# A two-layer encoder on one core: bias diagonals laid out during the value chunks, value loads and the last head's mixing placed differently

## The chip, the core and the metric

The kernel runs on one core of a Trainium2 chip. The metric is the device time of one execution in microseconds (us). The engines are PE (matrix multiplications and transposes into PSUM banks), DVE and POOL (elementwise work), ACT (activations, copies; it also issues DMAs from its own queue) and SP (issues DMAs only). Each engine executes its instructions in the order in which the program hands them over.

## What is computed

S = D = 1024, one batch, fp32. Each layer is `x <- x + RMSNorm_post(mixer(RMSNorm_pre(x)))`. Layer A is the part that the change touches, with 16 heads of width 128 and chunks of 128 positions:

```
z = h @ w_in                        # (1024, 3*2048)
u, v, g = split(z, 3)
u = gelu(u)
v = layer_norm(gelu(v), vn_g, vn_b)
vc = v.reshape(chunks, 128, 16, 128)
sg = einsum('hpq,cqhd->cphd', w_s, vc) + b_s    # mixing of positions
y = u * sg * silu(g)
return y @ w_out
```

Layer B is dilated window attention with a relative-position bias. The bias of a (query, key) pair depends on their distance alone, so the kernel makes one vector `vec` per head and lays it out 128 times in DRAM tensors `toep0`, `toep1`, `toep2`, from which layer B later reads diagonals.

## The kernel before

Products of fp32 values are made of three matmuls on high and low parts ("hi", "lo"). Weights come through `Pieces`: SP loads a 128 x 512 piece into `raw` (L160), ACT copies the hi part into one of 8 buffers `wt` (L176), and DVE or POOL subtracts for the lo part (L178). Nearly every matmul has the line L270, activations have L285, two-operand DVE and POOL work L288, fused DVE work L291.

The order of all work is written out by hand. `Plan` is a heap of steps with due times; its clock `plan.now` advances with each matmul by a modelled duration, and after each matmul of `dmm` all steps that are due are emitted, on whichever engine they belong to. `plan.after(dt, f)` places a step `dt` modelled microseconds ahead.

The stages, in real time of the profiled execution:

- 0 to 64: normalisation, and chunk 0 of the values (columns 0 to 511 of v). 64 to 202: value chunks 1 to 3, 8 pieces of weights each; their ends lie near 118, 163 and 203. At a chunk's end ACT evacuates eight PSUM banks into `vst` tiles (5 buffers) and SP stores each to `va` in DRAM (`va<-vst`, L107, 256 KB each).
- Into the chunks and the heads after them go 12 fills (`toep_fill`, L511): ACT issues one DMA, DRAM to DRAM, for four heads of one `toep` tensor: 768 KB (toep0), 1536 KB (toep1) or 512 KB (toep2).
- 202 to 555: 16 heads. Each head multiplies seven forms (a11, a12, s2, s1, s3, a22, s4) in that order; the weights of head h+1 are loaded in head h by `w_load` (L572): four SP loads `wb<-in_a_w_in` (b11, b21, b12, b22), then `w_sum` on POOL (t1 = b12 - b11, and three more), then hi and lo parts as pieces. Results are copied from PSUM by ACT (tiles `p`, `u`).
- Beside the multiplications of head h+1 runs the spatial part of head h: SP loads its values, 512 KB (`vr<-va`, L690), and the position weights come on ACT's queue (`wsr` L667, `bsr` L669); ACT normalises the values (L285, `vr`), ACT and DVE split them (`vs`), PE mixes in four steps (`mix`, `psS<-wst,vs`), DVE forms `sg` and `ya` (L291, L288), and SP stores `ya<-ya` (L725).
- From 555: the first output projection, whose pieces alternate between `ya` and `w_out`; the mixing of the last head lies in it. Then layer B, from 755 to the end.

Every SP or ACT transfer is assigned one of eight completion counters, in turn over both queues (`DMAHW0` to `DMAHW7` in the rows of the instruction order). An issue waits until the transfer that had its counter last has landed.

The steps that the change touches, with the lines of before:

```
plan.after(20.0 + 30.0 * (g + 3 * (h // 4)), toep_fill, g, h)   # the 12 fills
if pc.split < 32 + 7 * h:                                       # w_load
plan.at(t0, v_load)                                             # spatial
plan.at(t0 + 3.5 + 0.35 * i, v_norm, i)
plan.after(14.0, lambda: [f() for f in mixes])                  # last head
```

Of the kernel before, what the change touches and what calls it, by code (L numbers as in the profile page):

```python
# [12 lines left out]
F32 = mybir.dt.float32  # L13
# [8 lines left out]
P = 128  # L22
# [196 lines left out]
def encoder_block(ctx: ExitStack, tc: tile.TileContext, x, norm_pre, norm_post, a_w_in, a_w_s,  # L219
                  a_b_s, a_vnorm_g, a_vnorm_b, a_w_out, b_w_in, b_w_out, rel_bias, sel, out):  # L220
    nc = tc.nc
# [6 lines left out]
    plan = Plan()  # L228
# [12 lines left out]
    pc = Pieces(nc, plan, lambda: wpool.tile([P, 2, 512], F32R, name="wt"), 8)  # L241
# [136 lines left out]
    va = dram.tile([NH, P, 8, P], F32, name="va")  # L378
# [96 lines left out]
    for i in range(8):  # L475
        b = bank("D")
        for k in range(8):
# [5 lines left out]
            while n > 0 and norms:  # L483
                weight, f = norms.pop(0)
# [29 lines left out]

    for g in range(3):
        for h in range(0, NH, 4):
            plan.after(20.0 + 30.0 * (g + 3 * (h // 4)), toep_fill, g, h)

# [40 lines left out]

    def w_load(h):

        if pc.split < 32 + 7 * h:
            plan.after(0.5, w_load, h)
            return
        cols = a_w_in.shape[-1]
        B = {}
        for f, j, c0 in (("b11", 0, 128 * h), ("b21", 1, 128 * h), ("b12", 0, 2 * W2 + 128 * h),
                         ("b22", 1, 2 * W2 + 128 * h)):  # L570
            B[f] = fm.tile([P, 512], F32, name="wb", bufs=6)
            nc.sync.dma_start(B[f].rearrange("p (k n) -> p k n", k=4),  # L572
                              bass.AP(tensor=a_w_in.tensor, offset=a_w_in.offset + j * 512 * cols + c0,
                                      ap=[[cols, P], [128 * cols, 4], [1, 128]]))
        plan.after(3.0, lambda: w_sum(h, B, 0))
# [14 lines left out]
    for k in range(4):  # L590
        T = {}
# [32 lines left out]
    sp = sps.enter_context(tc.tile_pool(name="sp", bufs=2, side="right", reuse_waits="tile"))  # L624
# [35 lines left out]
    ws = {}  # L660

    def ws_load(h):

        if h < NH:
# [3 lines left out]
            T["b"] = sp.tile([P, P], F32, name="bsr")  # L668
            nc.scalar.dma_start(T["b"], bcast_row(a_b_s, h * P, P))  # L669

    def spatial(h, ug, t0):
        vs, T = {}, ws.pop(h)

        def ws_tr():
            b = bank("T")
            tr(b[:, :128], T["w"])
            T["wt"] = sp.tile([P, 2, P], F32R, name="wst")
            act(T["wt"][:, 0], b[:, :128])
            tt(T["wt"][:, 1], b[:, :128], T["wt"][:, 0].bitcast(F32), OP.subtract)

        def ws_sum():
            b = bank("T")
            bmm(b[:, :256], ones, T["wt"].rearrange("p a q -> p (a q)"), True, True)
            T["t2"] = sp.tile([P, P], F32, name="t2")
            stt(T["t2"], b[:, :128], vgb[:, 1, h:h + 1], T["b"], OP.mult, OP.add)
            stt(T["t2"], b[:, 128:256], vgb[:, 1, h:h + 1], T["t2"], OP.mult, OP.add)

        def v_load():
            vs["r"] = sp.tile([P, 8, P], F32, name="vr", bufs=1)
            nc.sync.dma_start(vs["r"], va[h])  # L690

        def v_norm(i):
            act(vs["r"][:, i], vs["r"][:, i], AF.Identity, scale=lnr[:, i:i + 1], bias=lnb[:, i:i + 1])

        def v_split(e):
            if e == 0:
                vs["v"] = sp.tile([P, 2, 8, P], F32R, name="vs", bufs=1)
                act(vs["v"][:, 0], vs["r"])
            else:
                tt(vs["v"][:, 1], vs["r"], vs["v"][:, 0].bitcast(F32), OP.subtract)  # L700

        def mix(cc):
            b = bank("S")
            for k in range(2):
                c = 2 * cc + k
                bmm(b[:, 256 * k:256 * k + 256], vs["v"][:, 0, c], T["wt"].rearrange("p a q -> p (a q)"),
                    True, False)
                bmm(b[:, 256 * k:256 * k + 256], vs["v"][:, 1, c], T["wt"].rearrange("p a q -> p (a q)"),
                    False, True)
            g = sp.tile([P, 2, P], F32, name="sg")  # L710
            b4 = b.rearrange("p (c a q) -> p c a q", c=2, a=2)
            t2 = T["t2"][:, None, :].to_broadcast([P, 2, P])
            stt(g, b4[:, :, 0], vgb[:, 0, h:h + 1], t2, OP.mult, OP.add)
            stt(g, b4[:, :, 1], vgb[:, 0, h:h + 1], g, OP.mult, OP.add)

            if cc == 0:
                vs["y"] = sp.tile([P, S], F32, name="ya", bufs=1)
            y = vs["y"].rearrange("p (t c b) -> p c t b", t=8, c=8)[:, 2 * cc:2 * cc + 2]
            tt(y, g.rearrange("p c (b t) -> p c t b", t=8),
               ug[:, 256 * cc:256 * cc + 256].rearrange("p (c b t) -> p c t b", c=2, t=8), OP.mult)  # L720
            if cc == 3:
                plan.after(2.0, y_out)

        def y_out():
            nc.sync.dma_start(ya[h], vs["y"])  # L725
            done_a.add(h)
            pc.pump()

        plan.at(t0, v_load)
        plan.at(t0 + 0.2, ws_tr)  # L730
        for i in range(8):
            plan.at(t0 + 3.5 + 0.35 * i, v_norm, i)
        plan.at(t0 + 6.5, v_split, 0)
        plan.at(t0 + 7.6, v_split, 1)
        plan.at(t0 + 6.2, ws_sum)
        plan.at(t0 + 7.6, ws_load, h + 2)
        return mix
# [68 lines left out]
    def head(h, mixes):  # L806
        if h + 1 < NH:
            plan.after(0.8, w_load, h + 1)
        u = sp.tile([P, S], F32, name="us")
        c0, c1 = slice(0, 512), slice(512, 1024)  # L810
        x, z, y = bank("D"), bank("O"), None
        g = {}

        def snap(nm):
            g[nm] = sp.tile([P, 512], F32, name=nm, bufs=1)
            act(g[nm], x)

        def gate(c, o, nm):

            g[c] = g[nm]  # L820
            tt(g[c], o, g[nm], OP.add)

        def gated(c, i):
            tt(u[:, c], u[:, c], g[i], OP.mult)

        form_mm(x, "a11", True)
        snap("p1")
        form_mm(z, "a12", True)
        tt(u[:, c0], z, g["p1"], OP.add)
        form_mm(x, "s2")  # L830
        snap("u2")
        y = bank("O")
        form_mm(y, "s1", True)
        form_mm(x, "s3")
        snap("u3")
        gate(1, y, "u3")
        for f in mixes[:2]:
            f()
        form_mm(x, "a22")
        act(u[:, c1], x, AF.Gelu_apprx_tanh)  # L840
        act(u[:, c0], u[:, c0], AF.Gelu_apprx_tanh)
        for f in mixes[2:3]:
            f()
        form_mm(y, "s4")
        gate(0, y, "u2")
        for f in mixes[3:]:
            f()
        for dt, c in ((0.0, 1), (0.9, 0)):
            plan.after(dt, act, g[c], g[c], AF.Silu)
        plan.after(1.4, gated, c1, 1)  # L850
        plan.after(2.4, gated, c0, 0)
        mix = spatial(h, u, plan.now + 0.5)
        return [lambda cc=cc: mix(cc) for cc in range(4)]

    mixes = []
    for h in range(NH):
        mixes = head(h, mixes)
    plan.after(14.0, lambda: [f() for f in mixes])
    fms.close()
    rps = ExitStack()  # L860
    rp = rps.enter_context(tc.tile_pool(name="rp", bufs=6, reuse_waits="tile"))
# [769 lines left out]
```

## Time and profile before

| what | value |
| --- | --- |
| median of three runs | 1989.4 us (1987.28 to 1990.86) |
| profiled execution | 1986.57 us |
| its span | 1984.8 us |
| PE busy | 1942.6 us, 98% |
| DVE, ACT, POOL busy | 67%, 55%, 17% |
| chain that ended last | PE 85%, DVE 6%, DMA 3%, ACT 3% |
| mean granted TensorE clock | 0.994 |

The views used are: the waits (which line of an engine stood idle for what, in total, how many times and the longest), the timeline of one engine in a window (start, duration, operation and, in brackets, the idle time ahead with what ended it), the chain of work that ended last, followed back from the end, a table by stretch of time (busy time of each engine, granted clock, DMA share and rate), and the DMA rate in slices of a window.

### The profile page before, as it was taken

Reading aid. Unit: us, or ns where it says so; the run is one execution under the profiler, and the core shown is the slowest. Engines: PE = TensorE matmul, PEld = TensorE weight load, DVE = VectorE, ACT = ScalarE, POOL = GpSimd, SP = SyncE. Lnnn points to the kernel's source line nnn. Section 1 sums busy time; section 2 is a strip of 40 time slices with the busy share of each in tenths; the row PEclk is TensorE's granted clock in tenths of the full one; section 3 lists DMA queues with packets and bytes.
Section 4 is the critical chain, followed back from the end, with each engine's and each line's share of the span. In section 5 each row is a group of like instructions: output and inputs, shape, how many; then the busy total and the mean of one; then the engine's idle time right before and its main releaser. Section 6 shows DMA issues by size and latency. Waiting matters only on the chain.

```text
span 1984.8 us, 30678 instructions
## 1 busy us (share of the span) xinstructions
PE 1942.6 (98%) x10617; PEld 1660.8 (84%) x10617; DVE 1326.7 (67%) x3051; ACT 1101.0 (55%) x2455; POOL 337.3 (17%) x394
## 2 busy tenths in 40 slices
PE   8999999999999999999999999999999999999998
PEld 5888787888778889988888888888888988787876
DVE  6455787888764777146576675676775756868647
ACT  5322566666645564246655656556556565675722
POOL 0001332232100000001131031120211300324032
PEclk9999999999999999999999999999999999999999
DMA  5342543443256775222232241322322322313277
GB/s 179 103 123 90 168 143 123 140 133 112 85 189 204 231 220 181 80 62 75 67 98 76 77 121 54 95 84 75 107 76 72 110 71 79 99 56 100 91 231 268
DMA packets 246024, 235.57 MB, mean 119 GB/s; under 512 B 18843, under 2 KB 203835, under 8 KB 245868
## 3 DMA queue, kind: packets, MB, share of 16 engines
q1 hardware_dynamic: 235068, 219.97, 36.2%
q10 hardware_dynamic: 10800, 13.63, 2.0%
q8 instruction: 84, 1.38, 0.3%
q14 instruction: 72, 0.59, 0.1%
HBM read 188.03 MB, written 57.04 MB: 123 GB/s over the span
## 4 chain that ended last, share of the span: by engine, by line
PE 85%; DVE 6%; DMA 3%; ACT 3%; issue 1%; POOL 1%; SPq 0%; ACTq 0%; DVEq 0%; POOLq 0%
PE psD L270 57%; PE psO L270 13%; PE psS L270 8%; PE psT L281 4%; PE psT L270 3%; DVE wt L178 1%; DVE o L288 1%; DMA vr<-va 1%; DMA va<-vst 0%; ACT wt L176 0%; DVE sg L291 0%; DMA raw<-in_b_w_in_dram 0%; DMA ya<-ya 0%; DVE xs L1157 0%; POOL o L288 0%
## 5 line engine op out<-in xcount | busy, mean ns | idle before, releaser
L270 PE MATMUL psD<-hTh,wt 128*128 128x512 f32 x2176 | 722.4, 396 | 5.7 <-ACT u L285 5.5
L270 PEld LDWEIGHTS psD<-hTh,wt 128*128 128x128 f32 x2176 | 401.1, 189 | 73.9 <-ACT u L285 6.6
L270 PE MATMUL psD<-hTl,wt 128*128 128x512 f32 x1088 | 433.1, 398 | 0.0
L270 PE MATMUL psD<-wt,hTh 128*128 128x256 f32 (+1 forms) x1760 | 357.1, 299 | 3.2 <-DVE wt L178 2.4
L178 DVE TENSOR_TENSOR wt<-raw,wt 128x512 fp32r<-128x512 f32 x316 | 210.1, 699 | 155.7 <-ACT wt L176 154.4
L270 PEld LDWEIGHTS psD<-wt,hTh 128*128 128x128 f32 x1760 | 281.9, 191 | 15.5 <-DVE wt L178 3.6
L285 ACT ACTIVATE xs<-xs,st 128x256 f32<-128x256 f32 (+2 forms) x384 | 176.7, 461 | 174.2 <-DVE st L1157 173.2
L176 ACT ACTIVATE wt<-raw 128x512 fp32r<-128x512 f32 x328 | 191.3, 624 | 144.3 <-PE psD L270 50.0
L270 PE MATMUL psD<-wt,hTl 128*128 128x256 f32 (+1 forms) x880 | 263.9, 300 | 0.8 <-DVE hTl L288 0.8
L270 PEld LDWEIGHTS psD<-hTl,wt 128*128 128x128 f32 x1088 | 205.3, 189 | 33.5
L270 PEld LDWEIGHTS psD<-wt,hTl 128*128 128x128 f32 x880 | 167.5, 190 | 6.3 <-DVE hTl L288 1.9
L288 DVE TENSOR_TENSOR pt<-psT,pt 128x512 fp32r<-128x512 f32 (+1 forms) x192 | 115.1, 600 | 85.5 <-ACT pt L285 82.8
L1157 DVE CUSTOM_DVE_ANT_0 xs<-psS,bias 128x256 f32<-128x256 f32 (+1 forms) x256 | 95.9, 412 | 61.6 <-PE psS L270 59.5
L1083 POOL TENSOR_SCALAR ks<-ks 64x512 fp32r<-64x512 f32 x96 | 59.6, 620 | 427.4 <-ACT ks L285 423.6
L288 DVE TENSOR_TENSOR ks<-psD,ks 64x512 fp32r<-64x512 f32 x96 | 66.1, 689 | 79.3 <-ACT ks L285 77.7
L270 PEld LDWEIGHTS psO<-pt,vs 128*128 128x128 f32 (+1 forms) x640 | 99.2, 177 | 23.5 <-DVE pt L288 7.2
L270 PE MATMUL psO<-pt,vs 128*128 128x256 f32 (+1 forms) x640 | 107.9, 282 | 4.6 <-DVE pt L288 3.5
L270 PE MATMUL psS<-ks,qs 128*128 128x256 f32 x640 | 109.8, 286 | 0.0
L285 ACT ACTIVATE pt<-psT 128x512 fp32r<-128x512 f32 (+1 forms) x192 | 99.9, 520 | 14.5 <-PE psT L281 11.6
L281 PE MATMUL psT<-ident,xs 128*128 128x128 f32 x640 | 103.6, 274 | 3.4 <-ACT xs L285 2.5
L270 PEld LDWEIGHTS psS<-ks,qs 128*128 128x128 f32 x640 | 97.9, 189 | 10.2 <-DVE ks L288 0.2
L285 ACT ACTIVATE ks<-psD 64x512 fp32r<-64x512 f32 x96 | 57.0, 593 | 80.7 <-PE psD L270 79.1
(218 smaller groups left out, 3191.3 us busy)
## 6 DMA issues: line engine op xcount, KB each, us to landing
raw<-in_b_w_in_dram SPq DMA_DIRECT2D x160, 256.0 KB, 3.0
wb<-in_a_w_in_dram SPq DMA_DIRECT2D x64, 256.0 KB, 6.4
raw<-ya SPq DMA_DIRECT2D x64, 256.0 KB, 3.0
raw<-in_a_w_out_dram SPq DMA_DIRECT2D x64, 256.0 KB, 4.0
y<-yd SPq DMA_DIRECT2D x56, 256.0 KB, 5.6
cb<-sc SPq DMA_DIRECT2D x64, 192.0 KB, 4.9
raw<-in_a_w_in_dram SPq DMA_DIRECT2D x32, 256.0 KB, 3.5
va<-vst SPq DMA_DIRECT2D x32, 256.0 KB, 3.9
```

Source lines behind the costliest of these rows:

```text
L176: self.nc.scalar.activation(hi, src, AF.Copy)
L178: e.tensor_tensor(lo, src, hi.bitcast(F32), op=OP.subtract)
L270: nc.tensor.matmul(o, l, r, start=start, stop=stop, skip_group_check=more)
L281: nc.tensor.transpose(o, i, ident)
L285: nc.scalar.activation(o, i, f, **k)
L288: (e or nc.vector).tensor_tensor(o, a, b, op=op)
L1083: nc.gpsimd.tensor_scalar(place(u, u.k[a][:, 0], o, o + 64, hh), hi.bitcast(F32), 1.0, 0.0, op0=OP.mult, op1=OP.add)
L1157: nc.vector.tensor_tensor_reduce(out=o, in0=s_, in1=bi, op0=OP.add, op1=OP.min, scale=1.0, scalar=3.0e38, accum_out=col(0, t))
```

## The change

Four edits. The 12 fills get due times 10 + 11.5 n after the start of chunk 1 in place of 20 + 30 n, so all of them are due within 136.5 modelled microseconds. `w_load` no longer waits for the pieces ahead of it where h is 0. The load of a head's values moves out of `spatial` into `head`, due 12 modelled microseconds after the head's start, and the normalisation and splitting of the values come 1.3 sooner. The last head's mixing is due 19 in place of 14 after the head's end.

```diff
-            plan.after(20.0 + 30.0 * (g + 3 * (h // 4)), toep_fill, g, h)
+            plan.after(10.0 + 11.5 * (g + 3 * (h // 4)), toep_fill, g, h)
...
-        if pc.split < 32 + 7 * h:
+        if h and pc.split < 32 + 7 * h:
...
+    vr = {}
+
+    def v_load(h):
+        vr[h] = sp.tile([P, 8, P], F32, name="vr", bufs=1)
+        nc.sync.dma_start(vr[h], va[h])
+
     def spatial(h, ug, t0):
-        vs, T = {}, ws.pop(h)
+        vs, T = {"r": vr.pop(h)}, ws.pop(h)
...
-        def v_load():
-            vs["r"] = sp.tile([P, 8, P], F32, name="vr", bufs=1)
-            nc.sync.dma_start(vs["r"], va[h])
...
-        plan.at(t0, v_load)
         plan.at(t0 + 0.2, ws_tr)
         for i in range(8):
-            plan.at(t0 + 3.5 + 0.35 * i, v_norm, i)
-        plan.at(t0 + 6.5, v_split, 0)
-        plan.at(t0 + 7.6, v_split, 1)
+            plan.at(t0 + 2.2 + 0.35 * i, v_norm, i)
+        plan.at(t0 + 5.2, v_split, 0)
+        plan.at(t0 + 6.3, v_split, 1)
...
     def head(h, mixes):
         if h + 1 < NH:
             plan.after(0.8, w_load, h + 1)
+        plan.after(12.0, v_load, h)
...
-    plan.after(14.0, lambda: [f() for f in mixes])
+    plan.after(19.0, lambda: [f() for f in mixes])
```

What the edits do to the order of instructions on each engine:

On ACT, at the end of value chunk 3 and the start of head 0, there stood before (the evacuations of the last two banks, the first form's copies, the position weights' loads, the copies of head 0):

```order
L285 ACTIVATE vst<-psD 128x512 [waits DMAHW5_49,DVE_49,PE_49]
L285 ACTIVATE vst<-psD 128x512 [waits DMAHW6_49,DVE_49,PE_49]
L285 ACTIVATE hTh<-s_699 128x512 x4
L667 DMA wsr<-in_a_w_s_dram 128x128
L669 DMA bsr<-in_a_b_s_dram 128x128
L667 DMA wsr<-in_a_w_s_dram 128x128 [waits DMAHW0_49]
L669 DMA bsr<-in_a_b_s_dram 128x128 [waits DMAHW2_49]
L285 ACTIVATE p_1656<-psD 128x512 [waits PE_49]
```

and now there stands, with the eleventh of the twelve fills, a toep1 of 1536 KB, in it:

```order
L285 ACTIVATE vst<-psD 128x512 [waits DMAHW3_49,DVE_49,PE_49]
L285 ACTIVATE vst<-psD 128x512 [waits DMAHW4_49,DVE_49,PE_49]
L511 DMA toep_99<-vec 512x1x768 [waits DMAHW0_49]
L285 ACTIVATE hTh<-s_699 128x512 x4
L667 DMA wsr<-in_a_w_s_dram 128x128
L669 DMA bsr<-in_a_b_s_dram 128x128 [waits DMAHW5_49]
L667 DMA wsr<-in_a_w_s_dram 128x128 [waits DMAHW7_49]
L669 DMA bsr<-in_a_b_s_dram 128x128 [waits DMAHW1_49]
L285 ACTIVATE p_1663<-psD 128x512 [waits PE_49]
```

Behind it only one more fill is left (toep2, in head 0); before, eight fills lay at or behind this place, in the heads.

On SP, from the last store of chunk 3 to the first value load, there stood before (`wb` are the four loads of head 1's weights):

```order
L107 DMA va<-vst 128x4x128 [waits DMAHW3_49,Activation_49]
L628 DMA vrow<-in_a_vnorm_g_dram 16x128 [waits DMAHW5_49]
L629 DMA vrow<-in_a_vnorm_b_dram 16x128 [waits DMAHW7_49]
L572 DMA wb<-in_a_w_in_dram 128x4x128 [waits DMAHW1_49]
L572 DMA wb<-in_a_w_in_dram 128x4x128 [waits DMAHW3_49]
L572 DMA wb<-in_a_w_in_dram 128x4x128 [waits DMAHW4_49,DVE_49,Pool_49]
L572 DMA wb<-in_a_w_in_dram 128x4x128 [waits DMAHW5_49,DVE_49,Pool_49]
L690 DMA vr<-va 128x1024 [waits DMAHW2_49,DMAHW6_49,DMAHW0_49,DVE_49]
```

and now:

```order
L107 DMA va<-vst 128x4x128 [waits DMAHW2_49,Activation_49]
L628 DMA vrow<-in_a_vnorm_g_dram 16x128 [waits DMAHW4_49]
L629 DMA vrow<-in_a_vnorm_b_dram 16x128 [waits DMAHW6_49]
L572 DMA wb<-in_a_w_in_dram 128x4x128 [waits DMAHW0_49]
L572 DMA wb<-in_a_w_in_dram 128x4x128 [waits DMAHW2_49]
L572 DMA wb<-in_a_w_in_dram 128x4x128 [waits DMAHW3_49,DVE_49,Pool_49]
L572 DMA wb<-in_a_w_in_dram 128x4x128 [waits DMAHW4_49,DVE_49,Pool_49]
L675 DMA vr<-va 128x1024 [waits DMAHW5_49,DMAHW1_49,DVE_49]
```

The transfers are the same and in the same order; the counters have shifted. The first load of head 1's weights now waits on counter 0, which the fill of ACT's row above was the last to be given; before it waited on counter 1, which a store of chunk 3 had last. The value loads of heads 0 to 13 and the loads of head 0's weights stand at the same places as before; the value load of head 14 stands one transfer sooner, that of head 15 six `raw` loads sooner.

On PE, in the first output projection, the last head's mixing (`psS<-wst,vs`) moves behind 24 more matmuls of the projection:

```order
+L270 MATMUL psD<-wt 128x512 x6
+L270 MATMUL psO<-wt 128x512 x6
+L270 MATMUL psD<-wt 128x512 x6
+L270 MATMUL psO<-wt 128x512 x6
L270 MATMUL psD<-wt 128x512 x4
L270 MATMUL psS<-wst,vs 128x256 x16
L270 MATMUL psD<-wt 128x512 x2
-L270 MATMUL psO<-wt 128x512 x6
-L270 MATMUL psD<-wt 128x512 x6
-L270 MATMUL psO<-wt 128x512 x6
-L270 MATMUL psD<-wt 128x512 x6
```

No other matmul changes its place. POOL's order is unchanged; on DVE four `wt` subtractions of the projection now stand ahead of the last head's `sg` steps.

## Rows read from the trace of the kernel before

**Rows 1.** The page: busy time of the engines.

```profile
PE 1942.6 (98%) x10617; PEld 1660.8 (84%) x10617; DVE 1326.7 (67%) x3051; ACT 1101.0 (55%) x2455; POOL 337.3 (17%) x394
```

**Rows 2.** PE's waits: total us, times, longest us.

```profile
PE psD L270 <- ACT u L285: 5.5, 3, 2.6
...
PE psD L270 <- ACT vst L285: 0.7, 2, 0.5
```

**Rows 3.** PE's timeline at the three waits for `u`: start, us, operation [idle before].

```profile
219.15 0.50 PE L270 MATMUL psD<-hTh,wt 128*128 128x512 f32 x1 [1.29 <-ACT u L285]
...
329.28 0.50 PE L270 MATMUL psD<-hTh,wt 128*128 128x512 f32 x1 [2.56 <-ACT u L285]
...
544.42 0.50 PE L270 MATMUL psD<-hTh,wt 128*128 128x512 f32 x1 [1.69 <-ACT u L285]
```

**Rows 4.** ACT's timeline in head 5, around a fill.

```profile
314.81 0.61 ACTq L511 DMA_DIRECT2D toep<-vec  x1
...
320.23 4.67 ACTq L667 DMA_DIRECT2D wsr<-in_a_w_s_dram  x1
```

**Rows 5.** The chain, 300 to 352: start, us, what.

```profile
329.28 4.38 PE psD L270 x12
...
348.93 2.77 PE psD L270 x12
```

**Rows 6.** By stretch: PE, PEld, DVE, ACT, POOL busy; clock, DMA share, GB/s.

```profile
330.00:335.00 5.00, 5.00 (x18) 4.05 (x18) 4.60 (x10) 2.35 (x4) 0.00 (x0) 0.66 0.40 139
575.00:580.00 5.00, 4.47 (x14) 3.79 (x15) 4.76 (x10) 0.00 (x0) 0.00 (x0) 0.52 0.55 174
```

**Rows 7.** The chain in head 14: the value load, and PE's piece after the third wait.

```profile
534.67 4.39 DMA vr<-va
...
544.42 3.04 PE psD L270 x12
```

**Rows 8.** SP's waits, whole span: what the `raw` load ahead of it waited for.

```profile
SPq L160 <- DVE wst L288: 20.3, 1, 20.3
```

**Rows 9.** PE's timeline around the last head's mixing.

```profile
569.58 0.28 PE L270 MATMUL psS<-wst,vs 128*128 128x256 f32 x1
570.52 1.09 PE L270 MATMUL psS<-wst,vs 128*128 128x256 f32 x7 [0.67 <-DVE vs L288]
575.14 1.19 PE L270 MATMUL psS<-wst,vs 128*128 128x256 f32 x4 [3.53 <-DVE sg L291]
...
580.51 1.54 PE L270 MATMUL psD<-wt 128*128 128x512 f32 x6
```

**Rows 10.** DVE's timeline in the same stretch.

```profile
570.39 3.69 DVE L178 TENSOR_TENSOR wt<-raw,wt 128x512 fp32r<-128x512 f32 x6
574.00 0.48 DVE L291 SCALAR_TENSOR_TENSOR sg<-psS,vgb,t 128x256 f32<-128x256 f32 x1
...
575.03 0.63 DVE L288 TENSOR_TENSOR ya<-sg,us 128x256 f32<-128x256 f32 x1
```

**Rows 11.** The chain at the ends of chunks 2 and 3: the stores.

```profile
155.11 6.89 DMA va<-vst
...
199.12 2.84 DMA va<-vst
...
202.07 0.60 ACT vst L285
```

**Rows 12.** The chain in head 0, from head 1's third weight load on.

```profile
209.51 3.40 DMA wb<-in_a_w_in_dram
```

**Rows 13.** DMA rate, 219 to 243, 0.6 us a slice, behind a fill issued at 219.57.

```profile
GB/s 0 0 51 271 155 103 77 97 87 102 108 108 108 102 102 102 108 102 102 102 108 108 108 102 102 102 119 182 128 135 93 187 260 373 341 334 351 300 212 160
```

**Rows 14.** SP's waits, 330 to 350, and its store of `ya` there.

```profile
SPq L725 <- DMA toep<-vec: 8.6, 1, 8.6
SPq L725 <- DVE wst L288: 3.2, 1, 3.2
...
340.53 0.34 SPq L725 DMA_DIRECT2D ya<-ya  x1
```

## The prediction

> **What bounds the kernel now.** The page first: PE is busy for 98% of the span [rows 1], so a change that removes no matmul can gain no more than PE's idle and slow-clocked pieces. Next the view of PE's waits, for what is idle in layer A: 5.5 us in three waits for ACT's copies `u`, and 0.7 us for `vst` at the ends of the value chunks [rows 2]. PE's timeline puts the three at 219.15 (1.29 us, head 0), 329.28 (2.56 us, head 5) and 544.42 (1.69 us, head 14) [rows 3]. The last head's mixing, at 570 to 580, is the fourth place, with waits of 0.67 and 3.53 us [rows 9]. Then the chain at each place, for what released it, and the table by stretch for the clock: behind two of these places it was granted at 0.66 and 0.52 on the mean of 5 us, a mixture of its two levels of 1.2 and 2.4 GHz, after stretches in which PE had stood idle [rows 6]. In the heads PE otherwise runs at 1.00 without gaps; the weights, values and position weights arrive behind it.
>
> **Part 1, fills out of the heads: the gain.** In head 5 ACT issued a fill at 314.81, and its next DMA issue, `wsr` at 320.23, then held ACT's queue for 4.67 us [rows 4]. Behind it stood the copies of weights and then `u`, for which PE waited 2.56 us [rows 3]. The 12 matmuls after that took 4.38 us, and the same 12 one head later 2.77 [rows 5]; the 1.61 between is the clock at 0.66. With no fill in head 5 both go: 2.56 + 1.61 = 4.2 us. Nothing is late next there, since the other heads without a fill at that place show no such wait in [rows 2].
>
> **Part 2, value loads.** The order of SP's transfers is unchanged through head 13, so "values sooner" and "first weights sooner" cost and gain nothing there. In head 14 the value load, 4.39 us long [rows 7], stood behind a `raw` load that waited 20.3 us [rows 8]; ACT's normalisation came late from it and `u` behind that, 1.69 us of PE [rows 3]. It now stands ahead of that load: 1.69 gone, and the 12 matmuls lose 3.04 - 2.77 = 0.27 us less (the piece at 544.42 [rows 7] against its usual length [rows 5]): 2.0 us. Normalising 1.3 sooner moves ACT work among ACT work with the same length: nothing.
>
> **Part 3, the last mixing.** From 569.58 to 580.51, 10.93 us, PE did 16 mixing matmuls and 8 of the projection [rows 9]. At full clock these take 16 x 0.12 + 8 x 0.2275 = 3.74 us (0.12 and 0.2275: 12 projection matmuls take some 2.75 us [rows 5], and mixing matmuls have half their columns). So 7.2 us are lost, idle and clock together. The 3.53 us are six `wt` subtractions of 3.69 us that DVE did ahead of the first `sg` [rows 10]. Moved 24 matmuls (5.5 us) later, the values are split well before the mixing and PE has no 0.67 us wait. What stays: PE can be two steps ahead of DVE (two banks psS), and one step is 0.48 + 0.48 + 0.63 us on DVE [rows 10] against 0.48 us on PE, so the third step waits for an `sg` pair (about 0.5 after PE's own second step), the fourth a further 1.1, and one or two subtractions may still be queued ahead (up to 1.0). That is 2.6 us left, 4.6 gained; between 1.5 (five subtractions ahead again) and 7.
>
> Gains together: 4.2 + 2.0 + 4.6 = **10.8 us**, 7.7 to 13.
>
> **Part 4, the ends of chunks 1 and 2: a cost.** Twelve fills now run nearly back to back from chunk 1 to head 0, since one alone moves at 102 to 108 GB/s [rows 13]. Beside a fill the store that frees the `vst` buffer took 6.89 us at the end of chunk 2, without one 2.84 us at the end of chunk 3 [rows 11]. The four microseconds showed as 0.7 us on PE in two waits [rows 2], since PE works on banks that are free. By the new order single stores of chunk 1 and of chunk 2 also wait for a fill's landing by its counter, which no row of before shows at this place. From below it costs nothing, if the fills have landed by then; from above a few us at each end, 5 together, as `SPq L725` once waited 8.6 us for a fill [rows 14]. I take the middle, **2.5 us**. The Trainium skill, "DMA: Bandwidth & Descriptors", section "Issuing engines are not separate DMA queues", says that transfers started by different engines run on the same 16 DMA engines and interleave; it speaks against moving fills beside stores, and were it not so this term would be nothing and the sum 2.5 us smaller. The two store durations side with it.
>
> **Part 5, head 0: the main cost.** The eleventh fill, 1536 KB, now stands on ACT's queue right behind the last `vst`, which in before ended at 202.07 + 0.60 [rows 11]; with the 2.5 us of part 4 and some queueing it is issued at about 206 (203 to 207). On SP the first load of head 1's weights is given the counter that this fill had last, and so waits until it has landed. Such a wait is real: in head 5's end the store `ya<-ya`, which neither reads nor writes `toep`, waited 8.6 us for a fill, and 3.2 us more for `wst`, before it was issued at 340.53; so the fill issued at 314.81 landed at 337.3, after 22.5 us [rows 4, 14]. From below: 1.573 MB at 105 GB/s is 15.0 us, and some 1.5 us pass before the rate rises [rows 13], so 16.5. The new place lies between: little else runs beside it while SP waits, but the last stores do. I take 19, landing at 225 (219.5 to 229.5).
>
> Behind the waiting load on SP stand the other three weight loads and head 0's values. POOL needs the third (b12); it is issued about 1.0 us after the first, lands after 3.4 us [rows 12], and from that landing, 209.51 + 3.40 = 212.91, to PE's a22 matmul at 219.15 [rows 3] there were 6.24 us of POOL differences, ACT copies and `u`. PE's order is fixed, so a22 of head 0 starts at 225 + 1.0 + 3.4 + 6.2 = 235.6 in place of 219.15: 16.4 later, of which 2.5 are part 4's. **+14 us** (11.5 to 17.5, by the fill's two lengths). Position weights that queue on ACT behind the fill, up to 4.67 us each [rows 4], lie inside this wait.
>
> The clock falls after so long a wait. What followed the 2.56 us wait cost 1.6 us (part 1); 5 us at 0.52, as behind the mixing [rows 6], would be 5 x 0.48 = 2.4. **+2.0 us**.
>
> Costs together 18.5 us, 13 to 25. The sum: -10.8 + 18.5 = **+7.7 us**, on the profiled execution 1986.6 + 7.7 = 1994.3. The profiled execution lies 2.8 us under the median, so the median would be 1989.4 + 7.7 = **1997.1 us**.
>
> **The rivals.**
>
> *Faster: the fill has landed when SP comes to the load.* Mechanism: counter 0 is free before head 1's weights are due. In before, SP came to its first weight load by about 207, and a delay of the third is covered only as far as POOL's wait allows; the 1.29 us wait at 219.15 [rows 3] says that there is no slack. So it decides at a landing by about 208 to 209; each later microsecond is one of PE. Then costs are part 4 and perhaps 1 us: -10.8 + 2.5 + 1 = -7.3, **1982 us** (1978 to 1985). For it: ACT could reach the fill sooner, and its rate could be higher when no head runs. Against it: every slice of a fill alone shows 102 to 108 GB/s [rows 13]; a landing at 208 from 203 needs three times that. 0.12. The Trainium skill gives this result by a formula ("DMA: Bandwidth & Descriptors", section "Anatomy of one DMA — SWDGE (gpsimd) path"): a DMA takes 2.0 us plus its bytes by 436e3 per us, an estimate of 5.6 us for this fill. The trace has three to four times as much.
>
> *No change: the gain and the stall cancel.* A fill of 16.5 us issued at 203, and no cost at the chunk ends: landing 219.5, PE at 230.1, +11 us, with 1.6 for the clock 12.6, less 10.8 to 13: **1990 us** (1986 to 1993). It needs all bounds on one side. 0.18.
>
> *It doesn't do what it says.* "Weights and values sooner" is empty in the order through head 13; that is in the sum already. The fills and the mixing do move.
>
> **How the numbers follow.** A difference under 0.2% (4 us) is about what a measurement of this kernel can't tell from none: faster is below 1985.4, slower above 1993.4. Forecast (slower) 0.70, its own range 1992 to 2006: gains from -12 to -8, costs 15 to 25. The other two 0.18 and 0.12. The range of 8 in 10, 1988 to 2006, leaves out the faster rival and the far end of the stall.
>
> **What the profile after would show.** Part 5 right: PE's waits have `psD <- ACT u` with a longest wait of 11 to 17 us in head 0, SP's waits have `L572 <- DMA toep<-vec`, and a slow clock stands behind it; POOL's first difference of head 1 starts at about 229. Wrong: that wait is near 1 us. Parts 1 and 2: no wait for `u` in heads 5 and 14. Part 3: the `sg` waits under 3 us and the clock near 1 behind the mixing. Part 4: `vst` waits of 1 to 5 us in all. The prediction is wrong above all if the weight load of head 1 isn't held, or if the fills delay each other so that the eleventh lands after 230.

## The result, and the profile after

The changed kernel takes 2001.08 us (median of 4 runs, 2000.61 to 2002.7), the kernel before 1988.39 us in the same series (4 runs, 1987.28 to 1990.86). The ratio is 1.006 with a 95% interval of 1.0048 to 1.0072: slower by 12.7 us. The forecast was 1997.1 us, 1988 to 2006, slower.

To see where the time went, the same PE instruction is looked up in both traces, stage by stage. The difference of its two start times is what the changed kernel has lost up to there.

| PE instruction | before | after | lost so far | in this stage |
| --- | --- | --- | --- | --- |
| first matmul of chunk 1 | 70.59 | 69.93 | -0.7 | |
| second piece of chunk 2 | 119.55 | 121.79 | +2.2 | +2.9 (end of chunk 1) |
| first matmul of head 0 | 201.82 | 207.92 | +6.1 | +3.9 (end of chunk 2) |
| transpose of head 0's position weights | 226.27 | 249.09 | +22.8 | +16.7 (head 0) |
| the same of head 5 | 338.38 | 356.95 | +18.6 | -4.2 (heads 1 to 5) |
| the same of head 15 | 555.67 | 572.62 | +17.0 | -1.6 (heads 6 to 15) |
| second part of the first projection | 607.73 | 619.99 | +12.3 | -4.7 (last mixing) |
| layer B, first group | 910.25 | 922.33 | +12.1 | -0.2 |
| end of the span | 1984.8 | 1999.4 | +14.6 | +2.6 |

Of the gain in heads 1 to 5, -4.4 us lie in head 5, and of that in heads 6 to 15, -1.9 lie in head 14; each of the other heads takes 0.03 us longer than before. ("Head 14" is, as in the prediction, the stretch around 544 in which the values of head 14 are worked on; PE is at the forms of the last head there.) Up to layer B this adds to 12.7 us from the start of chunk 1. That is the difference of the medians; the last 2.6 us of the profiled executions come almost wholly in the last 75 us and are taken up at the end.

The view of PE's waits after the change (what waited, for what: us in all, times, longest) answers to [rows 2]:

```profile
PE psD L270 <- ACT p L285: 7.9, 1, 7.9
PE psD L270 <- ACT u L285: 7.4, 1, 7.4
...
PE psD L270 <- ACT vst L285: 3.6, 4, 1.8
...
PE psS L270 <- DVE sg L291: 2.1, 2, 1.2
```

The waits for `u` in heads 5 and 14 are gone, `sg` lost nearly half. In their place stand 15.3 us in head 0, in two waits, and 3.6 us for `vst` (and 0.6 more in front of bank psO) where there were 0.7. SP's waits name what it waited for at the weight loads of heads 0 and 1:

```profile
SPq L572 <- DMA toep<-vec: 19.1, 2, 17.2
```

The chain of work through head 0 (start, us, what):

```profile
208.18 20.89 DMA toep<-vec
...
229.51 3.40 DMA wb<-in_a_w_in_dram
...
234.38 1.09 POOL tw L288
...
239.02 0.60 ACT u L285
...
239.67 5.49 PE psD L270 x12
```

It reads as part 5 put it: the fill is issued at 208.18 and lands at 229.07, then the weight loads go out, 3.40 us for the third of them, POOL's differences, the copies, `u`, and PE's a22 at 239.67. The forecast had 206, 225 and 235.6. ACT's timeline shows the first of PE's two waits:

```profile
208.18 0.60 ACTq L511 DMA_DIRECT2D toep<-vec  x1
...
209.23 8.28 ACTq L667 DMA_DIRECT2D wsr<-in_a_w_s_dram  x1
...
220.92 0.60 ACT L285 ACTIVATE p<-psD 128x512 f32<-128x512 f32 x1 [9.89 <-DMA bsr<-in_a_b_s_dram]
```

The load of `wsr` behind the fill held ACT's queue for 8.28 us (4.67 in [rows 4]), so `p` came late and PE stood; the work it did between that wait and the next shortened the second wait. By stretch (the number after POOL's is the clock), both waits are followed by matmuls at about the lower level of the clock, 1.2 GHz:

```profile
221.00:226.00 5.00, 4.43 (x12) 3.53 (x13) 0.69 (x1) 0.52 (x1) 0.00 (x0) 0.56 0.31 115
226.00:231.00 5.00, 5.00 (x23) 3.77 (x21) 0.00 (x0) 0.60 (x1) 0.00 (x0) 1.00 0.27 87
...
240.00:245.00 5.00, 5.00 (x13) 3.84 (x13) 3.32 (x4) 0.55 (x1) 1.39 (x1) 0.50 0.39 127
```

At the ends of chunks 1 and 2 the chain goes through a store that took 8.29 and 9.09 us, where [rows 11] had 6.89 and, without a fill beside it, 2.84:

```profile
111.95 8.29 DMA va<-vst
```

```profile
157.42 9.09 DMA va<-vst
```

Behind the second of them the clock was low for some 3 us (by stretch):

```profile
167.00:170.00 3.00, 2.74 (x7) 2.16 (x8) 2.58 (x4) 0.84 (x3) 0.00 (x0) 0.56 0.51 159
```

### The profile page after: what moved, and what is told of

Read it like the earlier page. It is cut to its first block, busy times and chain, and to the rows that moved or that the text cites. A ratio compares the mean times of both kernels' runs of the same rounds, so it can differ in the third digit from the quotient of the medians.

```text
span 1999.4 us, 30674 instructions
## 1 busy us (share of the span) xinstructions
PE 1944.7 (97%) x10617; PEld 1660.7 (83%) x10617; DVE 1320.9 (66%) x3051; ACT 1103.2 (55%) x2455; POOL 338.4 (17%) x394
## 4 chain that ended last, share of the span: by engine, by line
PE 86%; DVE 5%; DMA 5%; ACT 2%; issue 1%; POOL 1%; SPq 0%; DVEq 0%; ACTq 0%; POOLq 0%
PE psD L270 57%; PE psO L270 13%; PE psS L270 8%; PE psT L281 4%; PE psT L270 3%; DMA toep<-vec 1%; DMA va<-vst 1%; DMA y<-yd 1%; DVE wt L178 1%; DVE o L288 1%; DMA raw<-in_b_w_in_dram 1%; DMA raw<-in_a_w_in_dram 0%; DVE xs L1159 0%; DMA cb<-sc 0%; DVE qs L291 0%
## 5 line engine op out<-in xcount | busy, mean ns | idle before, releaser
L270 PEld LDWEIGHTS psD<-wt,hTh 128*128 128x128 f32 x1760 | 282.3, 191 | 18.4 <-ACT vst L285 6.0
```

Of the source, the lines that this page charges most:

```text
L270: nc.tensor.matmul(o, l, r, start=start, stop=stop, skip_group_check=more)
```

## The experiments

All twelve kernels are compared with the kernel before in series of their own, in which its median was 1986.8 to 1987.2 us. The table gives, by stage and against the trace of before, what each lost or gained, and the difference of the medians. "Chunk ends" is all that lies between the first matmul of chunk 1 and that of head 0; the columns of head 5 and head 14 hold that one head alone. A stage in which the clock fell in one of the two executions and not in the other differs by 1.6 us or so for that alone.

| kernel | chunk ends | head 0 | head 5 | head 14 | last mixing | medians |
| --- | --- | --- | --- | --- | --- | --- |
| the change | +6.8 | +16.7 | -4.4 | -1.9 | -4.7 | +12.7 |
| x1_fills_back | -0.1 | -0.6 | +2.6 | -2.0 | -4.7 | -3.9 |
| x2_fills_only | +6.6 | +15.1 | -4.4 | 0.0 | +0.8 | +19.0 |
| x3_mix_only | -0.1 | +0.2 | -1.6 | +4.1 | -0.1 | +3.0 |
| x4_loads_only | 0.0 | -0.4 | +2.6 | -2.0 | -4.7 | -4.1 |
| x13_loads_late_norm | -0.1 | -0.3 | -1.5 | -2.0 | -3.1 | -6.3 |
| x5_fill_wide | +0.2 | +4.8 | -4.4 | -2.0 | -4.7 | -5.7 |
| x6_back_wide | -0.3 | +0.3 | -4.4 | -2.0 | -3.1 | -11.2 |
| x7_fill11_quarter | +5.7 | +3.6 | -4.4 | -2.0 | -4.7 | +1.5 |
| x8_vst6 | +4.3 | +16.1 | -4.4 | -2.0 | -3.0 | +9.7 |
| x9_fill11_late | +6.8 | +1.0 | -4.4 | -2.0 | -3.1 | -4.5 |
| x10_fill_pool | +8.8 | +0.6 | -4.4 | -1.9 | -3.2 | -0.5 |
| x12_wide_early | -0.5 | -0.2 | -4.4 | -2.0 | -4.7 | -13.7 |

### Which edit carries what: x1 to x4 and x13

x1: the change with the fills put back.

```diff
-            plan.after(10.0 + 11.5 * (g + 3 * (h // 4)), toep_fill, g, h)
+            plan.after(20.0 + 30.0 * (g + 3 * (h // 4)), toep_fill, g, h)
```

> The change with the 12 fills put back to their due times of before (20 + 30 n); the value loads, the first weights and the later mixing of the last head stay as changed. Theory (the fills carry all the cost: about 6.8 us at the ends of chunks 1 and 2, 16.7 us in head 0, and the gain of 4.4 us in head 5): head 0 and the chunk ends look as before, head 5 waits for u again, and only heads 14 (-1.9) and the last mixing (-4.7) differ from before: 1988.4 - 6.6 = 1982, with PE's wait for ACT u in head 0 near 1.3 us. Rival (the loads that were moved hold up SP in head 0, not the fills): PE's waits of 7 to 8 us in head 0 stay, 1995 to 1999.

Measured: 1982.92 us, ratio 0.9979 (0.9969 to 0.9989). Head 0 and the chunk ends are as before, so the moved loads don't hold up head 0. One thing was not expected: head 5 is worse than in the kernel before by 2.6 us.

x2: the kernel before with the fills of the change alone.

```diff
-            plan.after(20.0 + 30.0 * (g + 3 * (h // 4)), toep_fill, g, h)
+            plan.after(10.0 + 11.5 * (g + 3 * (h // 4)), toep_fill, g, h)
```

> The kernel before with the due times of the 12 fills as changed (10 + 11.5 n) and nothing else. Theory: all costs and the gain of head 5, without the gains of head 14 and of the mixing: 1988.4 + 6.8 + 16.7 - 4.4 = 2007.5 (2005 to 2010). Rival (the fills cost only together with the moved loads): 1984 to 1992.

Measured: 2005.84 us, ratio 1.0094 (1.0079 to 1.0109). The fills alone bring the cost, but for 1.6 us in head 0, and the gain of head 5.

x3: the kernel before with the last head's mixing later.

```diff
-    plan.after(14.0, lambda: [f() for f in mixes])
+    plan.after(19.0, lambda: [f() for f in mixes])
```

> The kernel before with the last head's mixing due 19 in place of 14, and nothing else. Theory (the place of the mixing alone gives its gain; the values' earlier load isn't needed, since 24 matmuls later they are there): 1988.4 - 4.7 = 1983.7, the wait for DVE sg under 2.5 us in all and no wait for vs. Rival (the gain needs the value load of head 15 six transfers sooner): within 1 us of before.

Measured: 1989.87 us, ratio 1.0008 (0.9999 to 1.0017). No gain: the rival stood. Its 4.1 us in head 14 are a wait of 3.1 us in place of 1.69 and the clock behind it (0.50 from 544 to 548, where before had 1.00); no edit touches the order of instructions at that place in this kernel, so this seems to be how far one execution's wait there differs from another's, which no run here tests. PE's timeline of x3 at the mixing, and DVE's ahead of it, against [rows 9, 10]:

```profile
582.40 1.19 PE L270 MATMUL psS<-wst,vs 128*128 128x256 f32 x4 [4.19 <-DVE sg L291]
```

```profile
572.05 3.70 DVE L178 TENSOR_TENSOR wt<-raw,wt 128x512 fp32r<-128x512 f32 x6
576.09 1.52 DVE L178 TENSOR_TENSOR wt<-raw,wt 128x512 fp32r<-128x512 f32 x2 [0.34 <-ACT wt L176]
580.03 1.31 DVE L178 TENSOR_TENSOR wt<-raw,wt 128x512 fp32r<-128x512 f32 x2 [2.42 <-ACT wt L176]
581.26 0.48 DVE L291 SCALAR_TENSOR_TENSOR sg<-psS,vgb,t 128x256 f32<-128x256 f32 x1
```

The mixing stands later, but so do four more subtractions ahead of `sg`. The split of the values is as late as before; the weight pieces queue behind it, and `sg` behind those.

x4: the change with the fills put back as in x1 and the mixing put back too, so that the value loads, the earlier normalisation and the first weights' condition remain.

```diff
-    plan.after(19.0, lambda: [f() for f in mixes])
+    plan.after(14.0, lambda: [f() for f in mixes])
```

> The kernel before with the value loads, the earlier normalisation and the first weights' condition as changed; fills and mixing as before. Theory: only head 14's wait for u goes (1.7 to 2.0 us), and the last mixing may gain its 0.7 us wait for vs: 1988.4 - 2 to 3 = 1986. Rival (values sooner helps every head, as the words of the change say): 1975 to 1984. Second rival (it does nothing that can be measured, or takes transfers of head 15 into the way): 1988 to 1990.

Measured: 1982.72 us, ratio 0.9981 (0.9972 to 0.999), no different from x1. That is in the range of the first rival, but not for its reason: of the heads only 5 and 14 differ from before by more than 0.7 us. x4 has the full gain at the last mixing without the mixing being moved. SP's timeline, and DVE's:

```profile
546.21 0.42 SPq L675 DMA_DIRECT2D vr<-va  x1
```

```profile
564.48 1.22 DVE L288 TENSOR_TENSOR vs<-vr,vs 128x1024 fp32r<-128x1024 f32 x1
565.62 2.49 DVE L178 TENSOR_TENSOR wt<-raw,wt 128x512 fp32r<-128x512 f32 x4
569.23 1.29 DVE L178 TENSOR_TENSOR wt<-raw,wt 128x512 fp32r<-128x512 f32 x2 [1.12 <-ACT wt L176]
570.44 0.48 DVE L291 SCALAR_TENSOR_TENSOR sg<-psS,vgb,t 128x256 f32<-128x256 f32 x1
```

The values of head 15 are asked for at 546.21, in the trace of before some 11 us later; so they are split at 564.48 (569.24 before), the pieces' subtractions run while PE still multiplies, and only 1.29 us of them lie ahead of `sg`.

x4 also shows the 2.6 us lost in head 5. Its ACT timeline there, against [rows 4]:

```profile
317.22 0.61 ACTq L511 DMA_DIRECT2D toep<-vec  x1
...
318.70 7.19 ACTq L667 DMA_DIRECT2D wsr<-in_a_w_s_dram  x1
```

With the normalisation sooner, its eight activations stand ahead of the fill, not behind it, so the fill is issued 1.5 us ahead of the load of `wsr`, not 5.4 us as before, and that load is then held for 7.19 us in place of 4.67.

x13: x4 with the old times of normalisation and splitting.

```diff
-            plan.at(t0 + 2.2 + 0.35 * i, v_norm, i)
-        plan.at(t0 + 5.2, v_split, 0)
-        plan.at(t0 + 6.3, v_split, 1)
+            plan.at(t0 + 3.5 + 0.35 * i, v_norm, i)
+        plan.at(t0 + 6.5, v_split, 0)
+        plan.at(t0 + 7.6, v_split, 1)
```

> x4_loads_only with the normalisation and the splitting of the values at their old times (3.5, 6.5, 7.6 after the head's step in place of 2.2, 5.2, 6.3): the values' loads alone. Theory (the loads' places on SP carry the gains of head 14 and of the last mixing, the earlier normalisation does nothing): the same 1.95 and 4.7 us as x4, 1982.7. Rival (the earlier normalisation gives the gain at the last mixing, since it puts the splitting of the values ahead of six weight pieces on ACT and DVE): the mixing loses as before, 1985 to 1988.

Measured: 1980.82 us, ratio 0.9965 (0.9952 to 0.9977). The `sg` waits are those of x4 (2.1 us in two waits) and head 14 gains the same 2.0; head 5's wait is back at 2.6 us. The last mixing gains 3.1 us in this trace and not 4.7, since the clock fell behind the same two waits (0.62 from 568 to 572; in x4 it stayed at 1.00); x6, x8, x9 and x10, which have the earlier normalisation, show the same 3.0 to 3.2. So the loads' places carry both gains, and the earlier normalisation gives nothing here.

### What makes the fills cost: x5 and x7 to x10

x7: the eleventh fill cut to a quarter at its place, the rest as a thirteenth fill later.

```diff
+        a, n = (0, VLEN[g]) if h < NH else (192, 576)
+        if (g, h) == (1, 12):
+            n = 192
+        h = min(h, 12)
...
+    plan.after(220.0, toep_fill, 1, NH)
```

> The changed kernel with the eleventh fill cut to a quarter of its columns (384 KB) at its place, and the other three quarters as a thirteenth fill in a later head; all other transfers and their counters at the place in question stay. Theory (SP's first load of head 1's weights waits for the landing of this fill and of nothing else): landing about 5 to 6 us after the issue at 208, PE's two waits in head 0 (15.3 us and the clock) shrink to 1 to 4 us: 2001.1 - 14 = 1987 (1984 to 1991). Rival (the older fills' backlog on the queue or the DMA rate as such holds head 0 up): less than half of that gain, above 1994.

Measured: 1988.74 us, ratio 1.0003 (0.9994 to 1.0012); head 0 loses 3.6 us in place of 16.7. PE's waits there are

```profile
PE psD L270 <- ACT p L285: 3.7, 1, 3.7
...
PE psD L270 <- ACT u L285: 1.1, 1, 1.1
```

The quarter landed after 9.9 us (207.96 to 217.84; 5 to 6 had been expected), and SP still waited 6.3 us for it, which now costs PE little: the wait for `u` is about that of [rows 3], and what is left is `p`, behind ACT's queue. The landing of this one fill decides.

x9: the eleventh fill due 50 later.

```diff
-            plan.after(10.0 + 11.5 * (g + 3 * (h // 4)), toep_fill, g, h)
+            plan.after(10.0 + (50.0 if (g, h) == (1, 12) else 0.0) + 11.5 * (g + 3 * (h // 4)), toep_fill, g, h)
```

> The changed kernel with the eleventh fill alone due 50 modelled microseconds later, in head 2. Theory: head 0 goes as in the kernel before, 16.7 us less: 2001.1 - 16.7 = 1984.4, and up to 4 us more if head 2 waits for something behind the fill, as head 5 did before. Rival (the first weights' and values' loads hold head 0 up): above 1994.

Measured: 1982.77 us, ratio 0.9979 (0.997 to 0.9988). Head 0 loses 1.0 us, the chunk ends still 6.8. The two costs are separate.

x8: six `vst` buffers.

```diff
-        t = vst[i, c] = vp.tile([P, 512], F32, name="vst", bufs=5)
+        t = vst[i, c] = vp.tile([P, 512], F32, name="vst", bufs=6)
```

> The changed kernel with six vst buffers in place of five; everything else as changed. Theory (at the ends of chunks 1 and 2 PE loses 6.8 us because ACT waits for a vst buffer whose store runs beside a fill for 7 to 9 us): each evacuation then waits for a store issued one evacuation earlier, so each of the two ends loses 0.7 to 1.5 us less: 2001.1 - 2 = 1999. Rival (SP's stores are held back by their counters until a fill has landed, and the buffer doesn't matter): within 0.5 us of the changed kernel in that stage.

Measured: 1996.75 us, ratio 1.0046 (1.0034 to 1.0059). The end of chunk 1 loses 1.9 us in place of 2.9 and that of chunk 2 nothing in place of 3.9, so it is the buffers, held by slow stores, that PE waits for there. The 4.3 us of the table contain 2.5 us that the changed kernel doesn't lose, at the end of chunk 3, where PE waits for `vst` behind a store of 5.87 us. The other thing that x8 shows was not planned. With one buffer more the completion counters fall differently: the wait for the eleventh fill goes to the second load of `wsr` on ACT, not to SP's first weight load. ACT's timeline of x8, SP's waits from 206 to 232 us, and PE's waits:

```profile
206.69 0.60 ACTq L511 DMA_DIRECT2D toep<-vec  x1
...
227.80 0.33 ACTq L667 DMA_DIRECT2D wsr<-in_a_w_s_dram  x1
```

```profile
SPq L572 <- DMA wsr<-in_a_w_s_dram: 11.2, 1, 11.2
```

```profile
PE psD L270 <- ACT p L285: 17.0, 1, 17.0
```

PE now has one wait of 17.0 us, for `p`, which stands behind that load on ACT, and head 0 costs 16.1 us, nearly what it costs in the changed kernel. Whoever is given the fill's counter waits; which engine it is changes with the order of other transfers. The wait is also handed on: SP's third weight load, the one that POOL needs, has the counter of the first `wsr` load, which was issued behind the fill at 207.44 and had landed only at 228.0, 0.2 us after the fill. So in x8 SP's weights come no sooner either. In the changed kernel the third weight load has the same counter, so taking the fill's counter away from the first load alone need not have freed head 0.

x10: the fills issued from POOL's queue.

```diff
-        nc.scalar.dma_start(toep[g][h:h + 4],
+        nc.gpsimd.dma_start(toep[g][h:h + 4],
```

> The changed kernel with all fills issued from POOL's queue in place of ACT's; same places in the plan, same bytes, same form. POOL's transfers have completion counters of their own, so no load or store of SP or ACT is given a counter that a fill had. Theory (counters and ACT's queue carry the cost, not the bytes beside other transfers): head 0 as before (-16.7), the ends of chunks 1 and 2 keep what the shared DMA engines cost, 0 to 3 of 6.8 us: 2001.1 - 16.7 - 5 = 1979.5 (1976 to 1985). Rival (the fills' bytes slow the others): 1995 to 2002. Second rival (POOL's sums of the weights are held up behind the issue of a fill): a wait for POOL in some heads, 1985 to 1995.

Measured: 1986.77 us, above the range, ratio 0.9999 (0.999 to 1.0008). Head 0 is free (+0.6), but that doesn't test the counters: POOL issued the eleventh fill already at 181.76, and it landed at 201.19, 8 us before head 0 begins (the DMA view from 181 to 202 us, with its time to landing at the end):

```profile
toep<-vec POOLq DMA_DIRECT2D x1, 1536.0 KB, 19.4
```

And 9.3 us are lost at a place that no theory named, at the start of chunk 1. POOL's timeline, the DMA queues from 68 to 92 us, and the chain there:

```profile
55.31 7.69 POOL L511 DMA_DIRECT2D toep<-vec  x7 [40.54 <-DMA vec<-vect]
```

```profile
q0 software_dynamic: 3485, 5.43, 68.4%
...
toep<-vec POOLq DMA_DIRECT2D x1, 1536.0 KB, 28.4
```

```profile
66.92 12.66 DMA raw<-in_a_w_in_dram
```

On ACT a fill keeps its place because the activations around it wait for PE. POOL has nothing to wait for in the chunks, so seven fills go out at once, as soon as `vec` is there, and an eighth at 68.17. From 68 to 92 us they take 68.4% of all the DMA engines, and a 256 KB weight load takes 12.66 us.

x5: the fills' dimensions exchanged, so that the outer one is the 128 rows, not the 4 heads.

```diff
-        nc.scalar.dma_start(toep[g][h:h + 4],
-                            vec[h:h + 4, VOFF[g]:VOFF[g] + VLEN[g]].unsqueeze(1).to_broadcast(
-                                [4, P, VLEN[g]]))
+        src = vec[h:h + 4, VOFF[g]:VOFF[g] + VLEN[g]]
+        n = VLEN[g]
+        nc.scalar.dma_start(toep[g][h:h + 4].rearrange("h p n -> p h n"),
+                            src.unsqueeze(1).to_broadcast([4, P, n]).rearrange("h p n -> p h n"))
```

> The changed kernel with each fill's dimensions exchanged, so that its outer dimension is the 128 rows and not the 4 heads; same bytes, same places, same queue. Theory (a fill takes 18 to 23 us because it runs on a quarter of the DMA engines, at some 105 GB/s; whoever waits for its counter or its bytes waits that long): the 1536 KB fill lands in 5 to 9 us, by about 215 in place of 229, and the ends of chunks 1 and 2 lose most of their 6.8 us: 2001.1 - 14 - 5 = 1982 (1978 to 1987). Rival (the rate is set by the reads that repeat one vector or by the size of the pieces, not by the number of engines): the fill takes as long as before, 1999 to 2003.

Measured: 1981.53 us, ratio 0.9969 (0.9957 to 0.998). The DMA view of head 0 and ACT's timeline:

```profile
toep<-vec ACTq DMA_DIRECT2D x1, 1536.0 KB, 8.9
```

```profile
202.73 5.80 ACTq L668 DMA_DIRECT2D wsr<-in_a_w_s_dram  x1
```

The same bytes land in 8.9 us, with other transfers beside them, in place of 20.9; the ends of chunks 1 and 2 cost nothing any more, and of head 0's 16.7 us 4.8 are left, the wait for `p` behind ACT's queue. With four in the outer dimension a fill that runs alone has the DMA engines busy for 0.25 of the time, at 107 GB/s (x10, 192 to 200 us); while the wide fill runs the view puts the share at 1.02, at 309 GB/s, other transfers included (x5, 202 to 210 us).

### Two versions: x6 and x12

x6 is the change with the fills put back as in x1 and their dimensions exchanged as in x5.

```diff
-            plan.after(10.0 + 11.5 * (g + 3 * (h // 4)), toep_fill, g, h)
+            plan.after(20.0 + 30.0 * (g + 3 * (h // 4)), toep_fill, g, h)
...
-        nc.scalar.dma_start(toep[g][h:h + 4],
+        nc.scalar.dma_start(toep[g][h:h + 4].rearrange("h p n -> p h n"),
```

> x1_fills_back (fills at 20 + 30 n, in the chunks and in the heads) with the fills' dimensions exchanged as in x5_fill_wide. Theory (a fill that lands in under 10 us is out of the way of the position weights and the other loads in head 5): the wait for u in head 5, 2 to 5 us in the kernels with the fills there, shrinks to under 1 us: 1982.9 - 4 = 1979 (1976 to 1982). Rival (a fill on all the engines slows the head's weight and value loads more than one on a quarter of them): 1983 to 1990, with waits for u or wt in heads.

Measured: 1975.89 us, a little under the range, ratio 0.9938 (0.9925 to 0.9952). Head 5's wait is gone although the fills lie in the heads. The fill stands 1.5 us ahead of the load of `wsr`, as in x4, and that load is not held any more:

```profile
320.66 0.34 ACTq L668 DMA_DIRECT2D wsr<-in_a_w_s_dram  x1
```

x12 is x5 with all fills ahead of the end of chunk 3.

```diff
-            plan.after(10.0 + 11.5 * (g + 3 * (h // 4)), toep_fill, g, h)
+            plan.after(8.0 + 9.5 * (g + 3 * (h // 4)), toep_fill, g, h)
```

> x5_fill_wide with the fills due 8 + 9.5 n, so that the last one stands ahead of the evacuations of chunk 3 and none is left for head 0. Theory (what x5 still loses in head 0, 4.8 us in the wait for p, is ACT's queue behind the eleventh fill): 1981.5 - 4.8 = 1976.7 (1974 to 1980), no wait for u and none for p over 1.3 us. Rival (the loss in head 0 comes from the loads' places or from the stores of chunk 3): 1980 to 1983.

Measured: 1973.42 us, a little under the range, ratio 0.9937 (0.9923 to 0.9951): the lowest median, 13.7 us under the kernel before, but not to be told from x6, whose interval is the same and whose executions (1973.05 to 1977.31) lie among those of x12 (1972.77 to 1977.72). What the change wants, fills out of the heads at no cost, is there with this form of the fills. PE's waits (the one for `u` is that of head 0, 1.29 us in [rows 3]):

```profile
PE psD L270 <- ACT u L285: 1.6, 1, 1.6
...
PE psD L270 <- ACT p L285: 0.7, 1, 0.7
```

## Why the prediction was right, and where it was not

**Direction and cause: right.** The cost was forecast at the place, by the mechanism and on the engines where it came: the eleventh fill, its counter, SP's first load of head 1's weights, then 10.6 us to PE's a22 (229.07 to 239.67; 10.6 forecast). x7 and x9 show that it is that fill's landing, x8 that the wait goes where its counter goes. One sign did not come as written: the longest wait for `u` is 7.4 us, not 11 to 17, since PE had stood 7.9 us for `p` before it.

**Part 1 (-4.2 forecast, -4.4 measured)** holds; x2 has it with the fills alone.

**Part 2 (-2.0, -1.9)** holds for head 14. Its second half does not: "Normalising 1.3 sooner moves ACT work among ACT work with the same length: nothing" is true only where no fill stands in between; with the fills in the heads it costs 2.6 us of wait in head 5 (5.2 in x4 against 2.6 in x13).

**Part 3 (-4.6, -4.7): the right size from the wrong edit, which is luck.** The step that failed is "moved 24 matmuls later, the values are split well before the mixing and PE has no 0.67 us wait". It gave the gain to the mixing's place and counted the value load of head 15, six transfers sooner, at nothing. x3 has the place alone and gains nothing; x4 and x13 have the load without the place and gain it, 4.7 and 3.1 us. The 4.7 also needs a clock that stays at 1.00 behind the two waits that are left; where it fell (x6, x8, x9, x10, x13) the gain is 3.0 to 3.2. The row that should have told it was in hand: six `wt` subtractions directly behind the late split of the values [rows 10]. They are a backlog which that split made, and moving the mixing moves more subtractions in front of it.

**Part 4 (+2.5 forecast, 0 to 5; +6.8 measured)** was mis-sized, and its 4.3 us are most of what the forecast lacks. The mean of a best and a worst case was taken, and the worst case was too small: 8.29 and 9.09 us for a store, and both ends were hit. A store beside a fill had taken 6.89 us before and shown as part of 0.7 us on PE; with stores 1.4 and 2.2 us longer PE waited 2.0 us at the first end and 2.2 at the second, and the rest of the 2.9 and 3.9 us lies in the matmuls directly around these waits, at the second end at the lower clock. By x8 the buffer is what PE waits for, by x5 the length of the fill beside the store. SP did wait for a fill's counter there too (`SPq L107 <- DMA toep<-vec`, 7.4 us in two waits), but in chunk 1 the four stores that PE's buffers hung on had been issued by 113.3, before that wait: their own duration did it.

**Part 5 (+14 + 2.0 forecast, +16.7 measured)** holds. The fill took 20.9 us (19 forecast) and was issued 2.2 us later, as the chunk ends cost more. What was put inside the wait, ACT's queue, was a wait of its own of 7.9 us, and the two together, 15.3, are about as long as the one that was forecast; with a fill that lands in 9 to 10 us head 0 still loses 3.6 to 4.8 (x7, x5), nearly all of it that wait.

**The rivals.** The fill's landing came at 229, not by 208, so the faster one fell. The formula of the Trainium skill that the prediction cites there ("DMA: Bandwidth & Descriptors", section "Anatomy of one DMA — SWDGE (gpsimd) path"), an estimate of 5.6 us for 1536 KB, stands on that page for DMAs that POOL issues, and this fill goes out on ACT's queue. But issued from POOL, the same fill took 19.4 us (x10); the formula is nearer to x5's 8.9 us. The 20.9 us belong to the fill's form, four heads in the outer dimension. "No change" needed chunk ends at no cost, and they cost 6.8 us.

**What stays open.** From 910 us on, the profiled execution of the changed kernel loses 2.6 us more than before, nearly all behind 1911, where PE waits 3.3 us in three waits for `y<-yd` (1.2 in one before). Behind 1911 x1 loses the same 2.5, the others between -0.5 and +1.0. No run settles whether that is the change or the execution; the medians, 12.7 us apart, need nothing of it.

## What to carry to other kernels

A transfer that is far off the critical path can still stop an engine: ask of every long DMA which later issue is given its completion counter, and what is queued behind that issue. Give a long transfer an outer dimension that spreads it over the DMA engines before looking for a better place for it: here the form took 18.4 us off the changed kernel (x5), and with it the two places of the fills can't be told apart (x6, x12). And when a stall shows a queue of other work in front of the waiting step, look for what piled it up before moving the step: the backlog moves along.

## What the runs showed of the hardware

- A 1536 KB fill from DRAM to DRAM took 20.9 us with 4 in its outer dimension and 8.9 us with 128, both issued from ACT's queue. From POOL's queue, with 4, it took 19.4 us (x10, issued at 181.76, at first beside a 768 KB fill), and 28.4 us when it was issued behind seven others, which with it took 68.4% of the DMA engines from 68 to 92 us.
- A DMA issue behind such a fill on the same queue was itself held: `wsr` came free 9.3 us after the fill was issued in the changed kernel (208.18 to 217.51) and 10.1 us after it in head 5 before, in both some 12 us before the fill had landed. Behind a wide fill it was held in x5 (6.8 us, 201.75 to 208.53) and not in x6 (0.34 us for the issue). The fill is not the only thing that holds it: in x12, with no fill under way and the eight stores of chunk 3 on the DMA engines, the issue of `wsr` took 3.06 us.
- The same two waits of PE, 1.19 and 0.89 us, left the clock at 1.00 in x12 and brought it down in x6, which is 1.6 us of difference at that place. The tables by stretch of x6 and of x12:

```profile
572.00:576.00 4.00, 3.11 (x11) 2.59 (x11) 3.79 (x8) 0.00 (x0) 0.00 (x0) 0.68 0.11 42
576.00:580.00 4.00, 4.00 (x17) 3.25 (x16) 1.92 (x3) 1.33 (x3) 0.00 (x0) 0.89 0.43 160
```

```profile
572.00:576.00 4.00, 4.00 (x20) 3.33 (x20) 3.86 (x9) 1.15 (x2) 0.00 (x0) 1.00 0.00 0
```
